# The mixer's projection by seven block products through DRAM, with two weight tiles' operands made later

## The chip, the cores and the metric

The kernel runs on one core of a Trainium2 chip. The metric is the device time of one execution in microseconds (us). The engines are named as in the profile: PE (TensorE), DVE (VectorE), ACT (ScalarE), POOL (GpSimd) and SP (SyncE, which here only issues DMAs).

## The reference

The kernel computes one decoder block on x of 1024 tokens by 1024 channels in float32, cut here to the part around the change:

```python
u = rms_norm(x, norm_mix)
u_ssm, q, k, v, f_logit, gate_logits = split(u @ w_in)
y = gelu(s5_ssm(u_ssm, ...))
a, b = split(y @ w_glu); out_a = a * sigmoid(b)
out_b = forgetting_attention(q, k, v, f_logit + b_forget) @ w_fox_o
gate_a, gate_b = split(sigmoid(gate_logits))
h = x + (gate_a * out_a + gate_b * out_b) @ w_mix_out        # the mixer
h = h + memory_cross_attention(rms_norm(h), rms_norm(mem), w_q, w_kv, w_o)
f_a, f_b = split(rms_norm(h) @ w_ffn_in)
h = h + (silu(f_a) * f_b) @ w_ffn_out
out = rms_norm(h, norm_final)
```

The mixer's projection is a product of a 1024 x 1024 matrix (the merged gates, called g below) and w_mix_out, 1024 x 1024. The forget-attention has 8 heads of 64 channels, the memory attention 4 heads over 256 memory tokens.

## The kernel before

Every product is made in fp32r with both operands split: `hi` is the rounded operand (an ACT cast), `lo` the rest (a subtraction on DVE, at places on POOL), and hi·hi + hi·lo + lo·hi are three matmuls. One matmul has a stationary tile of 128 x 128 and moves 512 columns.

The stages around the change run in this order. **Fox** (`Fox.run`) makes values, forget sums and the heads of the forget-attention. It stores the cumulated forget sums to `cum_d` (the high part `cch` and the low parts `cl`), and reads them back into the rows `hb` of each head's operands; the per-head weights `raw<-in_w_in` come in through a ring of four raw buffers of 128 x 1024 (`wpool`, tag `raw`). Ahead of these SP copies w_glu into `wg_d`. **GLU and w_fox_o** (`glu.rest(j)`, `fox_part(j)`, j = 0 to 7, each 128 channels): a fox_part has 2 halves of 512 tokens; PE multiplies the attention by w_fox_o, DVE multiplies the result by the gate `gb` and adds it to `sg`, which gives the merged row block g_j (channels in partitions), and the split of g_j gives `mT`. **Mixer** (`mix`): for each tile t of 128 tokens and each half of 512 output channels, 8 blocks of 128 channels times 3 matmuls go into one PSUM bank; DVE adds the bank to a half row of x and writes H[t]. The weights are split beside it. After mix(t, second half) for t = 4 to 7 come norm(0) to norm(3), which scale H[t] to `xs`, turn it by 8 PE transposes and split it into `u2`. Between the mixes the list `ahead(0..2)` is woven in: it makes operands for the feed-forward's weight tiles 1 to 3 (loads `wpr`, sums, splits `wph`/`wpl`) and stores them to `w_d` by DMAs that ACT issues. **Memory queries** (`mem_q`): 4 heads, 24 matmuls each for the first 512 tokens, with norm(4) to norm(7) woven in. The memory scores follow.

The feed-forward's output stage already multiplies by seven block products (Strassen's scheme): a 2 x 2 block matrix product by 7 products of sums of blocks, whose operands are stored to DRAM and read back raw, split on reading.

The functions write the work out in program order, and the tile framework's scheduler makes one fixed order of instructions per engine of it; `B.behind` holds an instruction behind another one. Each engine and each DMA queue works its own list in order; semaphores carry the dependencies. DMAs issued by SP use eight semaphores in turn, so that a DMA may wait until the one eight places before it has landed.

Of the kernel before, what the change touches and what calls it, by code (L numbers as in the profile page):

```python
# [19 lines left out]
P = 128  # L20
# [98 lines left out]
class Block:  # L119
# [190 lines left out]
def hybrid_block_kernel(ctx: ExitStack, tc: tile.TileContext, x, mem, norm_mix, w_in, b_forget,  # L310
# [30 lines left out]
    wg_d = B.dram.tile([4, P, 2 * D], F32, name="wg_d")  # L341
    glu = Glu(B, sh, yT, wg_d, gate_d)
    with tc.tile_pool(name="fox", bufs=1, reuse_waits="tile") as fp:
        fox = Fox(B, fp, sh, uT, w_in, b_forget[0], cum_d, rd_d, att_d)
        fox.run(y_d, yT, aT, w_glu, wg_d, [f for j in range(4) for f in glu.values(j)])
    glu.after = fox.maxima[NH - 2]
    with tc.tile_pool(name="st2", bufs=1, reuse_waits="tile") as s2:
        stage_tail(B, big, s2, sh, x, glu, aT, gate_d, kv_d, w_fox_o, w_mix_out, norm_mem_q[0], w_mem_q,
                   w_mem_o, norm_ffn[0], w_ffn_in, w_ffn_out, norm_final, out)
# [232 lines left out]
def stage_tail(B, big, s2, sh, x, glu, aT, gate_d, kv_d, w_fox_o, w_mix_out, g_mq, w_mem_q, w_mem_o, g_ffn,  # L582
# [18 lines left out]
    mT = Act(s2, "t", NS2, 8, L, name="mx")  # L601
    fox = {}

    def fox_part(j):
# [6 lines left out]
        for h in range(2):  # L611
# [6 lines left out]
            mh, ml = mT.rhs(j, h)  # L618
            merged.append(B.split(mh, ml, sg[:, cs]))

    merged = []
# [21 lines left out]
    def wslots(src, pool_lo):  # L643

        nk = src.shape[0] // P
        raw = B.wpool.tile([P, RAW], F32, tag="raw", bufs=4, name="raw")[:, :D]
        S.dma_start(raw.rearrange("p (k c) -> p k c", k=nk), src.rearrange("(k p) c -> p k c", p=P))
        hl = bslot(F32R, "wbh"), bslot(F32R, "wbl")
        B.split(*hl, raw, pool_lo)
        return [t_.rearrange("p (k c) -> p k c", k=nk) for t_ in hl]  # L650

    def mix_weights(c):

        wm = ([], [])
        for kk in range(4):
            if c == 0:
                hl = B.wblock(w_mix_out, 2 * kk, 2, 0, 512)
            else:
                hl = wslots(w_mix_out[2 * kk * P:(2 * kk + 2) * P, 512:D], False)
            for w_, t_ in zip(wm, hl):  # L660
                w_ += [t_[:, 0, :], t_[:, 1, :]]
        return wm

    def mix(t, c, wm):
        cs = slice(512 * c, 512 * c + 512)
        ps = B.bank()
        gemm_n(ps, mT, t, wm, 8)
        V.tensor_add(H[t][:, cs], ps, load(x[t * P:(t + 1) * P, cs], "xr"))

    def norm(t, gb, act):  # L670
        xs = s2.tile([P, D], F32, tag="xs", bufs=1, name="xs")
        B.norm_scale(xs, H[t], B.rstd(H[t]), gb)
        return B.norm_turn(xs, act, t)
# [6 lines left out]
    def ahead(j):  # L680
# [14 lines left out]
        def plain():  # L695
            hl, _ = pair(0)
            with B.behind(merged[-1]):
                B.split(*hl, pre[j][0])
# [37 lines left out]
    wm0 = mix_weights(0)  # L736
    with B.behind(merged[-1]):
        wm1 = mix_weights(1)
    mixes = [lambda t=t: mix(t, 0, wm0) for t in range(NT)] + [lambda t=t: mix(t, 1, wm1) for t in range(4)]
# [15 lines left out]
    weave([lambda h=h: mem_q(h, 0) for h in range(MH)], [lambda t=t: normed.append(norm(t, gq, u2)) for t in range(4, 8)])  # L755
# [252 lines left out]
    gs = {}  # L1008
# [569 lines left out]
class Fox:  # L1578
# [280 lines left out]
    def run(self, y_d, yT, aT, w_glu, w_d, filler):  # L1859
# [131 lines left out]
```

## Time and profile before

| what | value |
|---|---|
| median of 3 runs | 1540.81 us (1539.42 to 1541.27) |
| profiled execution, span | 1538.1 us |
| granted TensorE clock over the span | 0.999 |
| last gated tiles end, mixer starts (PE) | 679.81 us |
| mixer's last matmul, memory queries start | about 770.6 us |
| norm(7)'s transposes on PE | 795.33 to 796.36 us |
| DVE, ACT, POOL busy, share of the span | 65%, 43%, 16% |

The page of the profiled execution gives no time of its own beside the span; the span runs from the first to the last instruction, and the median of the runs is 2.7 us above it. In the timeline a row has its start in us, its length, the engine, the line of the program, the operation, the tile written and those read, the shapes, the number of instructions, and in brackets the idle time before it with what ended it. In a group's row stand the total busy time and the mean in ns, then the idle time before. In the windows each engine has its busy time in us and its number of instructions.

### The profile page before, as it was taken

What the parts mean: (1) busy time and instruction counts of PE and PEld (TensorE: products, weight loads), DVE (VectorE), ACT (ScalarE), POOL (GpSimd) and SP (SyncE); (2) the same over time, 40 slices, a digit from 0 to 9 for tenths busy, and PEclk for the clock granted to TensorE, in tenths of its full rate; (3) what the DMA queues carried; (4) which work ended last, traced back from release to release, by engine and by line L of the source; (5) the groups of instructions that cost most, each with busy time, mean ns of one, the idle gap of its engine ahead of it and who ended that gap; (6) DMA issues with size and microseconds to landing.
All of it is one profiled execution on the core that took longest, in us unless ns stands there. A gap on an engine that the chain in (4) does not pass through costs nothing. (4 is left out here: it accounts for less than half of the span.)

```text
span 1538.1 us, 20434 instructions
## 1 busy us (share of the span) xinstructions
PE 1520.7 (99%) x7329; PEld 1257.7 (82%) x7329; DVE 1005.7 (65%) x1828; ACT 658.1 (43%) x1183; POOL 253.6 (16%) x341
## 2 busy tenths in 40 slices
PE   8999999999999999999999999999999999999998
PEld 7888888898777678888888888888888888888886
DVE  7936554355878867675556797777777775675555
ACT  7423334324667643232435663333333333354343
POOL 1166542100121214100102200000000000101001
PEclk9999999999999999999999999999999999999999
DMA  9634556611223746378210356555544544896542
GB/s 286 161 104 102 131 128 144 180 41 16 50 46 88 192 131 198 111 218 308 89 69 1 117 204 210 162 161 160 158 158 157 157 145 139 291 391 220 192 163 110
DMA packets 196293, 234.06 MB, mean 152 GB/s; under 512 B 35576, under 2 KB 127656, under 8 KB 195680
## 3 DMA queue, kind: packets, MB, share of 16 engines
q1 hardware_dynamic: 188704, 214.93, 47.0%
q10 hardware_dynamic: 7488, 17.83, 3.1%
q8 instruction: 57, 0.93, 0.3%
q14 instruction: 44, 0.36, 0.1%
HBM read 161.94 MB, written 72.71 MB: 153 GB/s over the span
## 5 line engine op out<-in xcount | busy, mean ns | idle before, releaser
L184 DVE TENSOR_TENSOR wlo<-raw,whi 128x1024 fp32r<-128x1024 f32 (+2 forms) x120 | 126.3, 1058 | 45.4 <-ACT whi L183 44.2
L183 ACT CAST whi<-raw 128x1024 fp32r<-128x1024 f32 (+2 forms) x120 | 108.7, 910 | 105.6 <-PE mm L174 39.1
L184 DVE TENSOR_TENSOR ol<-or,oh 128x1024 fp32r<-128x1024 f32 x73 | 90.1, 1236 | 74.0 <-ACT oh L183 71.9
L173 PE MATMUL mm<-uh,whi 128*128 128x512 f32 x344 | 136.5, 397 | 0.0
L174 PE MATMUL mm<-ul,whi 128*128 128x512 f32 x344 | 135.1, 393 | 0.0
L175 PE MATMUL mm<-uh,wlo 128*128 128x512 f32 x344 | 134.5, 391 | 0.0
L183 ACT CAST oh<-or 128x1024 fp32r<-128x1024 f32 x73 | 76.9, 1054 | 105.0 <-PE mm L1108 34.2
L997 POOL TENSOR_TENSOR g<-a,c 128x512 f32<-128x512 f32 x22 | 35.7, 1621 | 389.0 <-ACT a L996 389.0
L175 PEld LDWEIGHTS mm<-uh,wlo 128*128 128x128 f32 x344 | 64.7, 188 | 13.3 <-DVE wlo L184 0.2
L1803 POOL TENSOR_TENSOR pl<-pf,ph 128x512 fp32r<-128x512 f32 (+1 forms) x32 | 36.8, 1152 | 232.5 <-DVE ph L1802 193.3
L173 PEld LDWEIGHTS mm<-uh,whi 128*128 128x128 f32 x344 | 64.8, 188 | 11.6
L174 PEld LDWEIGHTS mm<-ul,whi 128*128 128x128 f32 x344 | 64.8, 188 | 11.0
L1800 ACT ACTIVATE pf<-sc 128x512 f32<-128x512 f32 (+1 forms) x96 | 46.4, 489 | 44.5 <-DVE sc L1796 28.3
L986 DVE SCALAR_TENSOR_TENSOR c<-c,pv 128x512 f32<-128x512 f32 x22 | 15.1, 687 | 76.5 <-ACT c L985 76.4
L211 POOL TENSOR_TENSOR r<-ms,mhalf 128x1 f32<-128x1 f32 (+1 forms) x26 | 15.7, 605 | 298.6 <-DVE ms L207 258.5
L964 PE MATMUL pv<-S3h,we 128*128 128x512 f32 x176 | 57.7, 389 | 0.0
L1806 DVE TENSOR_TENSOR pl<-pf,ph 128x512 fp32r<-128x512 f32 (+2 forms) x64 | 35.3, 553 | 10.4 <-ACT ph L1805 9.8
L1108 PE MATMUL mm<-ol,oh 128*128 128x512 f32 (+1 forms) x110 | 41.9, 381 | 0.0
L1108 PE MATMUL mm<-oh,ol 128*128 128x512 f32 (+1 forms) x110 | 41.9, 381 | 0.0
L1108 PE MATMUL mm<-oh 128*128 128x512 f32 (+1 forms) x110 | 41.9, 381 | 0.0
L173 PE MATMUL sc<-uh,whi 128*128 128x512 f32 x104 | 40.8, 392 | 0.0
L173 PE MATMUL mm<-yh,whi 128*128 128x512 f32 x104 | 40.7, 392 | 0.0
(639 smaller groups left out, 4554.2 us busy)
## 6 DMA issues: line engine op xcount, KB each, us to landing
or<-c_d SPq DMA_DIRECT2D x77, 256.0 KB
wo<-in_w_ffn_out_dram SPq DMA_DIRECT2D x22, 512.0 KB
c_d<-g SPq DMA_DIRECT2D x44, 256.0 KB
t_d<-wo SPq DMA_DIRECT2D x44, 256.0 KB
or<-t_d SPq DMA_DIRECT2D x44, 256.0 KB
rawb<-in_w_ffn_in_dram SPq DMA_DIRECT2D x20, 512.0 KB
raw<-in_w_ffn_in_dram SPq DMA_DIRECT2D x20, 512.0 KB
raw<-in_w_in_dram SPq DMA_DIRECT2D x19, 512.0 KB
```

The source lines that it names most:

```text
L173: T.matmul(ps, lh, rh, start=first, stop=False)
L174: T.matmul(ps, lh, rl, start=False, stop=False)
L175: return T.matmul(ps, ll, rh, start=False, stop=last)
L183: cast = self.A.copy(hi, src)
L184: self.rest = (self.G if pool_lo else self.V).tensor_sub(lo, src, f32(hi))
L211: self.G.tensor_tensor(out=r, in0=v, in1=self.mhalf[:, 0:n], op=ALU.pow)
L964: T.matmul(ps, l_[:, k, :], r_, start=first and k == 0 and i == 0, stop=k == 3 and i == 2, skip_group_check=True)
L997: G.tensor_mul(g[:, 512:], a1, c1)
L1108: T.matmul(ps, l_[:, gi], r_[:, c0:c1], start=k == 0 and (p == NP - LAST if own else p == 0 and n in (1, 2, 7)), stop=p == NP - 1 and k == ...
L1800: self.exp = A.activation(pf[:, off:], ps[:, off:], AF.Exp)
L1803: G.tensor_sub(pl[:, off:], pf[:, off:], f32(ph[:, off:]))
L1806: self.left = V.tensor_sub(pl[:, off:], pf[:, off:], f32(ph[:, off:]))
```

## The change

The mixer's product is divided into 2 x 2 blocks: tokens 0 to 511 and 512 to 1023, even and odd blocks of 128 channels (a pair p is the blocks 2p and 2p+1), and output channels 0 to 511 and 512 to 1023. Seven products n of 4 pairs x 4 token tiles x 3 matmuls replace the eight. They go in the order 1, 6, 7, 5, 4, 2, 3; a step `m` is one product and one pair, 12 matmuls into four PSUM banks, and behind a product's fourth pair DVE adds its four banks into H (product 2 goes tile by tile). Below m0 is product 1 with pair 0, m3 product 1 with pair 3.

- The left operands (1, 2, 4 are blocks of g; 3, 5, 6, 7 sums of blocks, made by four DVE operations per pair in `merged_pair`) are stored raw to `mc_d` and read back; the splits into mT are gone.
- The right operands 4 to 7 are sums of weight blocks. `mix_sums` makes them at the start of `Fox.run`: 8 loads of 512 KB, 16 POOL additions of 128 x 512 and 16 stores of 256 KB to `mt_d`. The operands 1 to 3 are read from w_mix_out.
- `m_get` reads both operands of a step (256 KB each) into one raw buffer; ACT casts it as a whole, DVE makes the left operand's low half, POOL the right one's. It goes five steps ahead.
- H[t] is loaded with x (8 loads of 512 KB), in place of 16 half rows.
- ahead(0) stays beside the mixer. ahead(1) and ahead(2) move to the memory queries, between norm(4) and norm(7).

The first place is SP at the start of Fox. The rows are DMAs, target and source, with their shapes and the semaphores that they wait for (DMAHW is a DMA's landing). Before:

```order
L1891 DMA wg_d_2966<-in_w_glu_dram 128x1x2048 [waits DMAHW6_49]
L1663 DMA cum_d_81<-cch_3411 8x1024 [waits DMAHW7_49,Activation_49]
L1668 DMA cum_d_81<-cl_3414 8x512 [waits DMAHW0_49,DVE_49]
L1668 DMA cum_d_81<-cl_3417 8x512 [waits DMAHW1_49,DVE_49]
L1701 DMA raw_3599<-in_w_in_dram 128x8x64 [waits DMAHW2_49]
L1702 DMA raw_3599<-in_w_in_dram 128x8x64 [waits DMAHW3_49]
L1741 DMA hb_3267<-cum_d_81 2x1024 [waits DMAHW4_49,DMAHW1_49,DMAHW7_49,DMAHW0_49,Pool_49]
```

In the change, from the last wg_d on (the first rows of 24), and further down up to the cl stores:

```order
L1973 DMA wg_d_2966<-in_w_glu_dram 128x1x2048 [waits DMAHW6_49]
L588 DMA wmix_3308<-in_w_mix_out_dram 128x1024 [waits DMAHW7_49,DVE_49]
L588 DMA wmix_3309<-in_w_mix_out_dram 128x1024 [waits DMAHW0_49,DVE_49]
L588 DMA wmix_3320<-in_w_mix_out_dram 128x1024 [waits DMAHW1_49,DVE_49]
L592 DMA mt_d_2967<-wmix_3308 128x512 [waits DMAHW7_49,DMAHW2_49,Pool_49]
L592 DMA mt_d_2967<-wmix_3308 128x512 [waits DMAHW3_49,Pool_49]
L592 DMA mt_d_2967<-wmix_3309 128x512 [waits DMAHW4_49,DMAHW0_49,Pool_49]
L592 DMA mt_d_2967<-wmix_3309 128x512 [waits DMAHW5_49,Pool_49]
L588 DMA wmix_3321<-in_w_mix_out_dram 128x1024 [waits DMAHW6_49,DVE_49]
```

```order
L588 DMA wmix_3345<-in_w_mix_out_dram 128x1024 [waits DMAHW3_49,DMAHW2_49]
L592 DMA mt_d_2967<-wmix_3344 128x512 [waits DMAHW6_49,Pool_49]
L1745 DMA cum_d_81<-cch_3460 8x1024 [waits Activation_49]
L592 DMA mt_d_2967<-wmix_3344 128x512 [waits DMAHW5_49,Pool_49]
L592 DMA mt_d_2967<-wmix_3345 128x512 [waits DMAHW2_49,Pool_49]
L592 DMA mt_d_2967<-wmix_3345 128x512 [waits DMAHW7_49,Pool_49]
L1750 DMA cum_d_81<-cl_3463 8x512 [waits DMAHW0_49,DVE_49]
L1750 DMA cum_d_81<-cl_3466 8x512 [waits DMAHW1_49,DVE_49]
```

Loads and stores of the weight sums now stand between wg_d and the cl stores; the reads of hb come behind them.

The second place is DVE and PE at the mixer's start. `sg` and `gb` belong to fox_part, `s3` and `s24` to merged_pair, `moh` and `mol` are a step's high and low operands. DVE in the change, around the end of the gated tile 5 (its second half's multiply is the row with misc) and the start of tile 6 (the last row):

```order
L647 SCALAR_TENSOR_TENSOR s24_6772<-sg_6264 128x512 [waits DVE_49]
L629 TENSOR_TENSOR gb_6768<-gb_6768,misc_6755 128x512 [waits DMAHW7_49,DMAHW4_49,PE_49]
L684 TENSOR_TENSOR mol_6788<-raw_6784,moh_6787 128x512 [waits Activation_49]
L630 TENSOR_TENSOR sg_6384<-sg_6384,gb_6768 128x512 [waits DVE_49]
L684 TENSOR_TENSOR mol_6796<-raw_6792,moh_6795 128x512 [waits Activation_49]
L648 SCALAR_TENSOR_TENSOR s24_6772<-s24_6772,sg_6384 128x512 [waits DVE_49]
L684 TENSOR_TENSOR mol_6804<-raw_6800,moh_6803 128x512 [waits DMAHW4_49,Activation_49]
L184 TENSOR_TENSOR wlo_6815<-raw_6812,whi_6814 128x1024 [waits DMAHW6_49,Activation_49]
L629 TENSOR_TENSOR gb_6831<-gb_6831,pv_6818 128x512 [waits DMAHW0_49,PE_49]
```

and PE in the change, where m2 gives way to tiles 6 and 7:

```order
L693 MATMUL sc_6853<-moh_6803 128x512 [waits Activation_49]
L693 MATMUL sc_6853<-mol_6804,moh_6803 128x512 [waits Pool_49]
L693 MATMUL sc_6853<-moh_6803,mol_6804 128x512 [waits DVE_49]
L693 MATMUL sc_6854<-moh_6803 128x512
L693 MATMUL sc_6854<-mol_6804,moh_6803 128x512
L693 MATMUL sc_6854<-moh_6803,mol_6804 128x512
L693 MATMUL mm_6855<-moh_6803 128x512
L173 MATMUL pv_6818<-ath0_0_2955,whi_6814 128x512 [waits Activation_49]
```

Before, the tiles came first and the mixer whole behind them. Now m0, m1 and seven matmuls of m2 stand ahead of the 48 matmuls of tiles 6 and 7, the five others behind them, and then m3.

The third place is DVE at the end of the mixer. The four adds of the last product are the rows with h4 to h7; `u2l` is norm 3's split, `wpr` and `wpl` belong to ahead(1), `xs` of h4 is norm 4:

```order
L700 TENSOR_TENSOR h6_6720<-h6_6720,mm_6855 128x512 [waits PE_49]
L700 TENSOR_TENSOR h7_6721<-h7_6721,mm_6856 128x512 [waits PE_49]
L184 TENSOR_TENSOR u2l0_0_6730<-pv_7623,u2h0_0_6722 128x2x128 [waits Activation_49]
...
L789 TENSOR_TENSOR wpr_7673<-wpr_7673,wpr_7674 128x512 [waits DVE_49]
L184 TENSOR_TENSOR u2l3_0_6736<-pv_7632,u2h3_0_6728 128x2x128 [waits Activation_49]
...
L184 TENSOR_TENSOR wpl_7800<-wpr_7673,wph_7799 128x512 [waits Activation_49]
L231 SCALAR_TENSOR_TENSOR xs_7704<-h4_6718,r01_7709,gbc_6963 128x1024 [waits DVE_49]
```

Before, an add of one H and the split and xs of an earlier norm took turns there. Now four adds come in a row, and pieces of ahead(1) stand between the splits of norm 3 and the xs of norm 4.

The diff, cut to its core:

```diff
+    mt_d = B.dram.tile([8, 4, P, 512], F32, name="mt_d")
...
-        fox.run(y_d, yT, aT, w_glu, wg_d, [f for j in range(4) for f in glu.values(j)])
+        fox.run(y_d, yT, aT, w_glu, wg_d, [f for j in range(4) for f in glu.values(j)],
+                [lambda p=p: mix_sums(B, w_mix_out, mt_d, p) for p in range(4)])
...
+def mix_sums(B, w, mt_d, p):
+    w1, w2 = [B.wpool.tile([P, RAW], F32, tag="raw", bufs=4, name="wmix")[:, :D] for _ in range(2)]
+    for i, t_ in enumerate((w1, w2)):
+        B.S.dma_start(t_, w[(2 * p + i) * P:(2 * p + i + 1) * P, :])
+    b11, b12, b21, b22 = w1[:, :512], w1[:, 512:], w2[:, :512], w2[:, 512:]
+    for n, o, i in ((5, b11, b12), (7, b12, b22), (6, b22, b11), (4, b21, b22)):
+        B.G.tensor_add(o, o, i)
+        B.S.dma_start(mt_d[n, p], o)
...
-            mh, ml = mT.rhs(j, h)
-            merged.append(B.split(mh, ml, sg[:, cs]))
+        gs[j] = sg
+        if j % 2 == 0:
+            S.dma_start(mc_d[1, j // 2], sg[:, 512:])
+        else:
+            merged_pair(j // 2)
+
+    def merged_pair(p):
+        ge, go = gs.pop(2 * p), gs.pop(2 * p + 1)
+        a21, a11, a22, a12 = ge[:, :512], ge[:, 512:], go[:, :512], go[:, 512:]
+        s24, s3 = slot(name="s24"), sh.half("s3")
+        for n, a_ in ((2, a12), (4, a22)):
+            S.dma_start(mc_d[n, p], a_)
+        V.tensor_sub(s3, a11, a21)
+        V.tensor_sub(a21, a22, a21)
+        V.scalar_tensor_tensor(out=s24[:, :512], in0=a21, scalar=-1.0, in1=a11, op0=ALU.mult, op1=ALU.subtract)
+        V.scalar_tensor_tensor(out=s24[:, 512:], in0=s24[:, :512], scalar=-1.0, in1=a12, op0=ALU.mult,
+                               op1=ALU.subtract)
+        for n, a_ in ((6, s24[:, :512]), (7, s3), (5, a21), (3, s24[:, 512:])):
+            S.dma_start(mc_d[n, p], a_)
...
+    MORDER = (1, 6, 7, 5, 4, 2, 3)
+    mseq = [(n, p) for n in MORDER for p in range(4)]
+    def m_get(m):
+        n, p = mseq[m]
+        r_ = B.wpool.tile([P, RAW], F32, tag="raw", bufs=4, name="raw")[:, :D]
+        S.dma_start(r_[:, :512], mc_d[n, p])
...
+        S.dma_start(r_[:, 512:], src)
...
+        A.copy(hl[0], r_)
+        V.tensor_sub(hl[1][:, :512], r_[:, :512], f32(hl[0][:, :512]))
+        G.tensor_sub(hl[1][:, 512:], r_[:, 512:], f32(hl[0][:, 512:]))
+        mops[m] = hl
...
+    MAHEAD = 5
+    fox_part(5)
+    for m in range(3):
+        m_get(m)
+    for t in range(4, NT):
+        m_x(t)
+    fox_part(6)
+    m_step(0)
+    m_get(3)
+    m_get(4)
+    m_step(1)
+    for t in range(4):
+        m_x(t)
+    fox_part(7)
+    m_get(5)
+    m_get(6)
...
-    weave(mixes, [f for j in range(AHEAD_IN + 1) for f in ahead(j)], 4)
-    for t in range(4, NT):
-        mix(t, 1, wm1)
-        norm(t - 4, gq, u2)
+    weave([lambda m=m: m_next(m) for m in range(2, 20)], ahead(0), 4)
+    last = [lambda i=i: (m_tile(i), m_next(20 + i)) for i in range(4)] + [lambda m=m: m_step(m) for m in range(24, 28)]
+    weave(last, [lambda t=t: norm(t, gq, u2, ("pv", "pv")) for t in range(4)])
...
-    weave([lambda h=h: mem_q(h, 0) for h in range(MH)], [lambda t=t: normed.append(norm(t, gq, u2)) for t in range(4, 8)])
+    later = [f for j in range(1, AHEAD_IN + 1) for f in ahead(j)]
+    for f in later[:1]:
+        f()
+    turns = [lambda t=t: normed.append(norm(t, gq, u2)) for t in range(4, 8)]
+    weave([lambda h=h: mem_q(h, 0) for h in range(MH)],
+          [f for i in range(4) for f in turns[i:i + 1] + later[1 + 3 * i // 2:1 + 3 * (i + 1) // 2]])
```

More of the change, by code (lines that the diff above doesn't have):

```diff
@@ L641, in gemm_n, with norm @@
             B.mm3(ps, ah, al, w[0][k], w[1][k], k == 0, k == nk - 1)
[L643 to L670, printed above, removed]
+    def norm(t, gb, act, banks=("misc", "pv")):
         xs = s2.tile([P, D], F32, tag="xs", bufs=1, name="xs")
         B.norm_scale(xs, H[t], B.rstd(H[t]), gb)
-        return B.norm_turn(xs, act, t)
+        return B.norm_turn(xs, act, t, banks)
     AHEAD_IN = 2
@@ L696, in plain @@
             hl, _ = pair(0)
-            with B.behind(merged[-1]):
-                B.split(*hl, pre[j][0])
+            B.split(*hl, pre[j][0])
             for i, t_ in enumerate(hl):
```

75 lines of the change are left out of this document (59 added, 16 removed).

## The prediction

> **What bounds the kernel now.** I read the page's busy table and slices first.
>
> ```profile
> span 1538.1 us, 20434 instructions
> PE 1520.7 (99%) x7329; PEld 1257.7 (82%) x7329; DVE 1005.7 (65%) x1828; ACT 658.1 (43%) x1183; POOL 253.6 (16%) x341
> ...
> PEclk9999999999999999999999999999999999999999
> ```
>
> TensorE (PE) is busy for 99% of the span and its clock is granted in full in every slice; a microsecond taken from PE's own work is a microsecond of the kernel, unless something else is late there. So a change is worth the matmuls that it removes, less the new time in which PE stands still. Next I read the windows over the stages that the change touches (PE, PEld, DVE, ACT and POOL busy, clock, DMA share, GB/s) and one step of the chain of waits.
>
> ```profile
> 308.00:346.00 38.00, 38.00 (x267) 35.43 (x266) 19.54 (x56) 10.98 (x20) 0.00 (x0) 1.00 0.15 37
> 640.00:680.00 40.00, 40.00 (x178) 33.14 (x177) 29.12 (x37) 11.36 (x17) 6.00 (x4) 1.00 0.55 171
> 700.00:740.00 40.00, 40.00 (x178) 33.14 (x177) 20.88 (x30) 12.43 (x19) 0.56 (x1) 1.00 0.85 299
> 771.00:797.00 26.00, 25.92 (x131) 21.50 (x130) 13.32 (x29) 8.17 (x23) 0.55 (x1) 1.00 0.13 45
> 1346.00:1384.00 38.00, 38.00 (x169) 31.45 (x169) 27.77 (x27) 21.52 (x26) 2.51 (x2) 1.00 1.05 391
> 1054.62 2.72 PE mm L964 x12
> ```
>
> PE idles nowhere here: at the start of the forget-attention (308 to 346), beside the last gated tiles (640 to 680), in the mixer (700 to 740), among the memory queries (771 to 797). Twelve matmuls of 128x512 take 2.72 us, 0.2267 us each. The output stage (1346 to 1384) already does what the mixer is to do, seven products from DRAM, at 391 GB/s and without a gap.
>
> **What the change removes.** The mixer had 8 token tiles x 2 halves x 8 k x 3 = 384 matmuls; seven products x 4 pairs x 4 tiles x 3 are 336. 48 x 0.2267 = **10.9 us** of PE go. The 32 transposes stay, and so does every other matmul. Of the 16 merged splits, whose work was off PE's path, nothing is won.
>
> **Steady mixer: 0.** One step (12 matmuls, 2.72 us) needs two reads of 256 KB, one ACT cast of 128x1024, a half subtraction on DVE and one on POOL, and on average one DVE add into H.
>
> ```profile
> 709.24 1.05 ACT L183 CAST wph<-wpr 128x1024 fp32r<-128x1024 f32 x1 [7.31 <-DMA wpr<-in_w_ffn_in_dram]
> L986 DVE SCALAR_TENSOR_TENSOR c<-c,pv 128x512 f32<-128x512 f32 x22 | 15.1, 687 | 76.5 <-ACT c L985 76.4
> L1803 POOL TENSOR_TENSOR pl<-pf,ph 128x512 fp32r<-128x512 f32 x24 | 30.9, 1289 | 78.5 <-DVE ph L1802 73.0 <-DVE mboth L1776 5.6
> L1252 POOL TENSOR_TENSOR sg<-sg,ga 128x512 f32<-128x512 f32 x16 | 25.7, 1628 | 77.0 <-DVE sg L1245 49.8 <-DMA ga<-gate_d 27.2
> L1445 POOL TENSOR_TENSOR w<-la_re,cT_re 128x512 f32<-128x512 f32 x4 | 4.4, 1111 | 0.2
> ```
>
> That is 1.05 us of ACT, 2 x 0.69 = 1.4 of DVE and 1.3 to 1.6 of POOL in 2.72, and 524 KB / 2.72 us = 193 GB/s, under the 299 that the mixer's window moves now and the 391 of the output stage. PE's own step hides it; if that cover went (four raw buffers, each held for a read plus 1.05 + 1.3 us, feed a step in 2.72 us only while the read stays under 8.5 us), it would cost a rival's price, below. Taking the weights of feed-forward tiles 2 and 3 away from here makes it lighter, and I give that no gain since PE had no idle time there.
>
> **Place A, the start of the forget-attention: +5.3.** SyncE (SP) issues in order. It now has 8 loads of w_mix_out and 16 stores to mt_d between wg_d and the stores of cum_d that hb is read from. The first rows below are SP's, then DVE's, POOL's and PE's.
>
> ```profile
> 301.74 1.78 SPq L1891 DMA_DIRECT2D wg_d<-in_w_glu_dram  x2
> 339.96 0.87 SPq L1668 DMA_DIRECT2D cum_d<-cl  x2
> 342.14 0.26 SPq L1741 DMA_DIRECT2D hb<-cum_d  x1
> 343.39 0.24 SPq L1742 DMA_DIRECT2D hb<-cum_d  x1
> 322.31 1.23 DVE L184 TENSOR_TENSOR wlo<-raw,whi 128x1024 fp32r<-128x1024 f32 x1
> 374.71 0.74 POOL L1803 TENSOR_TENSOR pl<-pf,ph 128x256 fp32r<-128x256 f32 x1 [82.30 <-DVE ph L1802]
> 351.21 0.22 PE L1763 MATMUL pv<-hb 68*128 68x128 f32 x1
> 1.67 0.36 SPq L370 DMA_DIRECT2D xt<-in_mem_dram  x1
> 5.91 1.06 ACT L413 ACTIVATE junk<-xt 128x1024 bf16<-128x1024 f32 x1 [0.77 <-DMA xt<-in_mem_dram]
> 723.60 0.38 SPq L731 DMA_DIRECT2D wpr<-in_w_ffn_in_dram  x1
> 730.44 1.05 ACT L183 CAST wph<-wpr 128x1024 fp32r<-128x1024 f32 x1 [4.95 <-DMA wpr<-in_w_ffn_in_dram]
> ```
>
> SP was free from 303.5 on and POOL idle until 374.71, so pair 0 costs nothing. But its tiles come from the ring of four raw buffers, and pair 1's second load needs a buffer that DVE's split frees at 322.31 + 1.23 = 323.5. From there three pairs run one behind another: the second load of a pair stands on SP behind the stores of the pair before, lands 4.2 us later (5.91 - 1.67; under load 730.44 - 723.60 = 6.8), three POOL additions must follow it, and about 0.5 us of issues. An addition of this shape lies between 1.11 (L1445) and 1.63 (L1252); I take their mean, 1.37. A pair is 4.2 + 3 x 1.37 + 0.5 = 8.8, the last store goes at 323.9 + 3 x 8.8 = 350.3, and the two cl stores behind it. As before, the last hb read is issued 343.6 - 340.0 = 3.6 us later, at 353.9, and takes about 2.6 (an estimate, between the 2.2 from cum_d<-cl to hb<-cum_d and the 3.2 from rd_d to rb below). PE, whose order up to there is the same, wants hb at 351.2: 356.5 - 351.2 = 5.3. The ends: 3.6 us a load and 1.11 an addition give 7.3 a pair and +0.9; 6.8 and 1.63 give 12.2 a pair and +15.5. The DMA share of 0.15 puts it near the lower loads. Below nothing it can't go, since PE waits for nothing there now. Behind hb on SP stand the head weights (raw<-in_w_in), which PE needs later.
>
> [...]
>
> **Place B, the start of the mixer: +5.9.** PE now runs m0, m1 and part of m2 ahead of the last gated tiles 6 and 7, and m3 right behind them.
>
> ```profile
> 573.96 0.32 SPq L1838 DMA_DIRECT2D rd_d<-rc  x1
> 577.16 0.47 SPq L1840 DMA_DIRECT2D rb<-rd_d  x1
> 599.73 0.32 SPq L597 DMA_DIRECT2D gb<-gate_d  x1
> 601.94 0.69 DVE L616 TENSOR_TENSOR gb<-gb,pv 128x512 f32<-128x512 f32 x1 [3.23 <-DMA gb<-gate_d]
> ```
>
> A store and the read that waits for it are 3.2 us apart (577.16 - 573.96). A 256 KB read is used 2.2 us after the last issue of its kind (601.94 - 599.73), and one of twice the size after 4.2; I take 2.9. Tile 6's second half ends 26 matmuls (5.9 us) into the run of 48; its multiply and add (2 x 0.69) end at 7.3, the read of its mc_d piece is issued at 10.5 and lands at 13.4, ACT's cast ends at 14.4, POOL's half at 15.7. PE is through with the 48 and the rest of m2 (53 x 0.2267) at 12.0, and can do 0.7 us of high parts before it needs POOL's half: 2.4 + 0.6 = 3.0. Before that, m0's low half stands on DVE behind the last multiply of tile 5 (2 x 0.69 = 1.4, of which PE has 0.9 to do: 0.7 with the hop), and the last w_fox_o load stands on SP behind a store that waits for tile 5's add: +0.8. Behind m3, m4 and m5 reuse the banks that four DVE adds (2.8 us) must empty, with two subtractions among them: +1.4. Sum 5.9. Low 2.5 (m3 alone, every transfer as short as the rows have it), high 12 (both reads at 6.8). Late next is nothing: m7 comes just in time, and from there the steady step has room to catch up.
>
> [...]
>
> **Place C, the memory queries: +1.7.** H[4] to H[7] used to be complete one by one; now all four wait for the last product.
>
> ```profile
> 769.77 0.69 DVE L668 TENSOR_TENSOR h<-mm,xr 128x512 f32<-128x512 f32 x1 [1.68 <-PE mm L175]
> 778.24 0.41 DVE L184 TENSOR_TENSOR u2l<-misc,u2h 128x256 fp32r<-128x256 f32 x1
> 778.57 1.27 DVE L231 SCALAR_TENSOR_TENSOR xs<-h,r,gbc 128x1024 f32<-128x1024 f32 x1
> ...
> L184 DVE TENSOR_TENSOR wpl<-wpr,wph 128x512 fp32r<-128x512 f32 x8 | 5.4, 685 | 7.9 <-DMA w_d<-wph 7.9
> L184 DVE TENSOR_TENSOR wpl<-wpr,wph 128x1024 fp32r<-128x1024 f32 x3 | 3.7, 1223 | 9.9 <-ACT wph L183 9.9
> ```
>
> DVE has four adds of 0.69 at the end of the last product and only behind them u2l of norm 3 (0.41): 3.2 us. PE wants it after 8 transposes and 4 matmuls, 1.8 us: +1.4. Then xs of norm 4 is ready after those 3.2 us, three pieces of u2l (1.2), two additions and two subtractions of the moved operands (4 x 0.69), some small ones and its own 1.27, about 8.7; PE, pushed back by 1.4, wants it 27 matmuls and 8 transposes after the last product (7.0) and so at 8.4: +0.3. The moved operands are two of the three tiles behind the two wpl rows, the second of them only in part: about half of 5.4, two of the three of 1.22 and five additions of 0.69 on DVE, 8.6 us in all, and as many casts on ACT; DVE's 13.3 us and ACT's 8.2 in the 26 us of this window leave room for them. Low 0.3 if DVE's queue is ahead; high 4.8 if a moved subtraction waits for a buffer of a w_d store as long as the 4.95 above, less what is in time.
>
> **Sum.** -10.9 + 0 + 5.3 + 5.9 + 1.7 = **+2.0 us**; the profiled span would be 1540.1. The median of the runs is 1540.8, 2.7 above the profiled span: **1543 us**, a little slower, within what can be told from nothing (0.2%, 3.1 us).
>
> **Rivals.**
> 1. *The new chains are all hidden.* Then -10.9 stands: 1530. For it: in the output stage the same step leaves no gap, and POOL and SP are idle around 310 to 340. Against it: three places where rows give a wait on PE's path. With two of the three places small (0.9 + 2.5 + 0.3) it is -7.2 and 1533.6.
> 2. *Only one of A and B stalls*, the other at its low end: -10.9 + 5.3 + 2.5 + 1.7 = -1.4 or -10.9 + 0.9 + 5.9 + 1.7 = -2.4: about 1539.
> 3. *Slower: the pairs' weight sums hold SP.* One mechanism at A: every further 0.9 us per pair is 2.7 us on hb; from 9.2 us a pair on, the sum is slower by over 0.2%. With the load of 6.8 and POOL at 1.63 it is +15.5, and the sum +12.2: 1553. For it: POOL's addition at 1.63 is the nearest in form. Against: DMA share 0.15.
> 4. *Slower: reads of the mixer's steps outlast 8.5 us* when loads of H, operands of tile 1 and w_d stores run beside them; a read of 10 gives 3.1 a step, 0.4 x 20 steps = 8 us, 1551. Against: 391 GB/s in the output stage.
> 5. *The change doesn't do what it says*, the count of matmuls not falling: 28 steps of 12 stand in the code against 384, so I give it nothing.
>
> **Chances.** Forecast (the sum, 1537 to 1549) 0.45; rival 1 0.22; rival 2 0.13; rival 3 0.12; rival 4 0.08. Faster by more than 0.2% (under 1537.7): all of rival 1, half of rival 2, a little of the forecast, 0.31. Slower (over 1543.9): rivals 3 and 4 and half of the forecast, 0.40. The rest, 0.29, is no change that can be measured. Range 1530 to 1554: from rival 1's end to just over rival 3's.
>
> **What would show it.** The page of the changed kernel should list 48 matmuls fewer and a PE busy time lower by 10.9. In the waits, PE L1763's counterpart should wait some 5 us for DMA hb near 351 (none: A was hidden; 10 or more: rival 3). PE's mixer steps should wait for ACT and POOL moh, mol within the first eight steps, 3 us at m3. Behind that, windows of the mixer with PE not full mean rival 4. Near the end of the mixer, PE should wait for DVE u2l and xs, under 2 us. What would make it wrong: SP issuing cum_d before 345, or a landing under 2 us.

## The result, and the profile after

The changed kernel takes 1568.3 us (median of 4 runs, 1563.4 to 1570.5) against 1540.1 before (4 runs, 1539.4 to 1541.3): a ratio of 1.0177, 95% interval 1.0159 to 1.0195. It is slower by 28 us where the sum of the prediction had 2. The profiled execution spans 1567.1 us. Its page:

```profile
span 1567.1 us, 20655 instructions
PE 1521.8 (97%) x7281; PEld 1253.3 (80%) x7281; DVE 1044.5 (67%) x1860; ACT 668.4 (43%) x1187; POOL 324.6 (21%) x385
```

PE has 48 matmuls fewer (7281 against 7329), as the change says. They were worth 10.9 us, yet PE's busy time has risen by 1.1: the matmuls that are left count 12 us more. The rest is waiting. The groups of PE's waits, over the whole program (total, times, longest):

```profile
PE mm L693 <- DVE h L700: 7.1, 1, 7.1
PE pv L1845 <- DMA hb<-cum_d: 5.4, 1, 5.4
PE misc L237 <- DVE u2l L184: 4.1, 1, 4.1
PE sc L693 <- DVE mol L684: 2.8, 2, 2.4
PE sc L693 <- ACT moh L683: 2.8, 1, 2.8
PE misc L1740 <- DVE logf L1727: 2.7, 1, 2.7
...
PE sc L693 <- POOL mol L685: 0.9, 1, 0.9
```

These seven sum to 25.8 us; a few shorter ones in the mixer and the queries (L693 and L237, 0.2 to 0.6 each) add 1.1. None of them was there before. So the span's +29.0 is, to 1.0 us: -10.9 removed, +26.9 of waits, +12.0 in PE's busy time. Of these 12, some 7.4 are a lower granted clock, right behind four of the waits (below and in the last section); the rest is not placed, but part of it is how busy time counts: a matmul ahead of a stop counts 0.39 us (the last ahead of the 7.1 us, at 756.07), one with the next behind it 0.2267. Windows of the mixer in the changed kernel (length, then busy time of PE, PEld, DVE, ACT and POOL, clock, DMA share, GB/s):

```profile
712.00:756.00 44.00, 43.21 (x187) 34.45 (x186) 39.98 (x45) 20.29 (x22) 26.88 (x16) 1.00 0.91 301
756.00:764.00 8.00, 0.91 (x4) 0.51 (x3) 4.68 (x7) 4.52 (x5) 7.40 (x6) 0.83 0.89 269
764.00:769.00 5.00, 5.00 (x15) 3.86 (x15) 3.98 (x10) 4.76 (x13) 2.13 (x2) 0.59 1.06 310
```

PE's own timeline where it starts again (start, duration, operation, in brackets the wait ahead of it and its releaser):

```profile
763.55 0.77 PE L693 MATMUL mm<-whi 128*128 128x512 f32 x1 [7.09 <-DVE h L700]
764.12 0.63 PE L693 MATMUL mm<-wlo,whi 128*128 128x512 f32 x1
764.55 0.63 PE L693 MATMUL mm<-whi,wlo 128*128 128x512 f32 x1
```

From 712 to 756 the steps run nearly full. Then PE stands for 7 us, and when it goes on its granted clock is 0.59: the starts are 0.43 us apart (764.55 - 764.12), not 0.2267, until 768.0. This wait thus cost some 2 us more than its length.

What PE waited for there is DVE, in its own timeline, beside POOL's and SP's:

```profile
752.90 4.09 DVE L684 TENSOR_TENSOR wlo<-raw,whi 128x512 fp32r<-128x512 f32 x3
757.55 1.11 DVE L684 TENSOR_TENSOR mol<-raw,moh 128x512 fp32r<-128x512 f32 x1 [0.56 <-ACT moh L683]
759.86 0.69 DVE L684 TENSOR_TENSOR mol<-raw,moh 128x512 fp32r<-128x512 f32 x1 [1.20 <-ACT moh L683]
762.12 0.69 DVE L684 TENSOR_TENSOR mol<-raw,moh 128x512 fp32r<-128x512 f32 x1 [1.57 <-ACT moh L683]
762.73 0.68 DVE L700 TENSOR_TENSOR h<-h,mm 128x512 f32<-128x512 f32 x1
...
751.14 6.97 POOL L685 TENSOR_TENSOR wlo<-raw,whi 128x512 fp32r<-128x512 f32 x4 [2.17 <-ACT whi L683]
...
752.99 0.32 SPq L670 DMA_DIRECT2D raw<-mc_d  x1
...
754.77 0.32 SPq L670 DMA_DIRECT2D raw<-mc_d  x1
```

The adds into H (L700) that free product 2's bank stand in DVE's list behind the low halves of three later steps, m24 to m26, whose operands only come in. DVE is not busy all that time: it waits 0.56, 1.20 and 1.57 us for ACT's casts, and ACT for the reads. The reads of m24 and m25 go at 752.99 and 754.77, just as POOL's halves of m20 and m21 (1.74 us each, 6.97 / 4) end and give their raw buffers back. And a low half of 128x512 on DVE, 0.69 us, takes 1.36 on the mean of the first row (4.09 / 3).

### The profile page after: what moved, and what is told of

It reads as the page before. It is cut to its first block, busy times and chain, and to the rows that moved or that the text cites. A ratio compares the mean times of both kernels' runs of the same rounds, so it can differ in the third digit from the quotient of the medians.

```text
span 1567.1 us, 20655 instructions
## 1 busy us (share of the span) xinstructions
PE 1521.8 (97%) x7281; PEld 1253.3 (80%) x7281; DVE 1044.5 (67%) x1860; ACT 668.4 (43%) x1187; POOL 324.6 (21%) x385
## 4 chain that ended last, share of the span: by engine, by line
PE 81%; DVE 8%; DMA 5%; ACT 2%; issue 2%; POOL 1%; SPq 0%; POOLq 0%; DVEq 0%; ACTq 0%
PE mm L1047 15%; PE pv L1047 8%; PE mm L173 7%; PE mm L174 7%; PE mm L175 7%; PE mm L1190 5%; PE sc L1047 4%; PE sc L1190 4%; PE pv L1190 3%; PE sc L175 3%; PE sc L174 3%; PE sc L173 3%; PE misc L1190 2%; DMA wpr<-in_w_ffn_in_dram 1%; PE sc L1875 1%
## 5 line engine op out<-in xcount | busy, mean ns | idle before, releaser
L184 DVE TENSOR_TENSOR wlo<-raw,whi 128x1024 fp32r<-128x1024 f32 (+2 forms) x116 | 122.4, 1060 | 40.4 <-ACT whi L183 39.6
L183 ACT CAST whi<-raw 128x1024 fp32r<-128x1024 f32 (+2 forms) x116 | 104.8, 907 | 99.2 <-PE mm L174 36.4
L685 POOL TENSOR_TENSOR mol<-raw,moh 128x512 fp32r<-128x512 f32 x24 | 40.1, 1686 | 40.8 <-ACT moh L683 40.6
L683 ACT CAST moh<-raw 128x1024 fp32r<-128x1024 f32 x24 | 25.0, 1050 | 51.6 <-DMA raw<-mc_d 26.8
```

Of the source, the lines that this page charges most:

```text
L183: cast = self.A.copy(hi, src)
L184: self.rest = (self.G if pool_lo else self.V).tensor_sub(lo, src, f32(hi))
L685: G.tensor_sub(hl[1][:, 512:], r_[:, 512:], f32(hl[0][:, 512:]))
```

## The experiments

Each is one execution with its profile unless said otherwise, beside the kernel before on the same chip. The changed kernel's own runs spread over 7 us, so a difference in total under that is not told from nothing, and the waits of the profile are what is compared.

**e1, the weight sums left out** (products 4 to 7 then read plain blocks of w_mix_out).

```diff
-                [lambda p=p: mix_sums(B, w_mix_out, mt_d, p) for p in range(4)])
+                [])
-            src = mt_d[n, p]
+            src = w_mix_out[2 * p * P:(2 * p + 1) * P, :512]
```

> The weight sums are left out: products 4 to 7 read plain blocks of w_mix_out (the right operands of four products are not sums, so the time holds and the values don't). Theory A (the sums on SP and POOL cost 10.9 us at the start of the forget-attention: logf 2.9, hb 5.6, slower matmuls behind them, the rest before): PE reaches the first attention matmul of w_fox_o within 2 us of the kernel before (592.8 to 594.8 in place of 603.7), no wait for logf or hb, and the total falls by 9 to 10 us against the changed kernel, to about 1558. Rival (the two waits come from something else, say the tile framework's order there): the waits stay and the total stays at 1568.

1555.7 us. PE reaches the first matmul of the attention by w_fox_o at 593.3 (592.8 before, 603.7 in the change); the waits for logf and hb are gone. Of the 10.4 us, 1.0 was there before the first of the two waits (PE was to come to logf's transposes at 336.7 in the change, at 335.7 in e1). So the sums cost some 9 us at the start of the forget-attention, as theory A has it. The mixer's wait in front of product 2 stays in e1 and e3, at 8.2 and 8.5 us: it has another cause.

**e2, the sums' transfers issued by POOL; e3, the transfers on SP and no POOL additions.**

```diff
 e2:
-        B.S.dma_start(mt_d[n, p], o)
+        B.G.dma_start(mt_d[n, p], o)
 e3:
-        B.G.tensor_add(o, o, i)
```

(In e2 the loads go the same way; in e3 mt_d then holds plain blocks.)

> The 8 loads and 16 stores of the weight sums are issued by POOL and not by SP; the additions stay on POOL. Theory A1 (two separate causes: SP's order holds cum_d and hb, 5.4 us; POOL's additions slow DVE's logf chain, 2.7 us): the wait for hb is gone (below 1 us), the wait for logf stays at 1.5 to 3 us; total about 1562. Rival A2 (the landing of the 24 transfers, not their place on SP, makes hb late): the wait for hb stays at 4 to 6 us. Rival A3 (DVE's logf chain is late by SP or by DMA, not by POOL): the logf wait goes too, total about 1558.

> The sums' loads and stores stay on SP, the 16 POOL additions are left out, so mt_d holds plain blocks (values are off, the transfers are the same). Theory A1: DVE's logf chain is as fast as before (the seven L1724 steps in 1.8 us, not 4.4) and the wait for logf is gone; hb, now 3 x 4 us earlier per chain of pairs, waits under 1 us; total about 1558. Rival A3 (logf is slowed by the transfers): the seven steps stay at 4 us and the logf wait at 2 to 3 us.

e2: 1574.0 us, worse, with the wait for hb at 6.7 us and the one for logf at 2.5. Its place on SP was free, but now another list was full: the small constant `ones` that DVE's scan of the forget sums reads is set by POOL, behind POOL's transfers and additions.

```profile
353.05 0.52 POOL L1736 MEMSET ones<- 8x512 f32 x1
353.60 1.21 DVE L1741 TENSOR_TENSOR_SCAN cum<-ones,misc 8x512 f32<-8x512 f32 x1 [12.90 <-POOL ones L1736]
```

So e2 does not tell A1 from A2 as it was meant to; it shows that the pairs' chain holds whatever is queued behind it. e3: 1555.0 us, waits of 0.8 us for hb and none for logf, with all 24 transfers still ahead of the cl stores on SP, which go at 345.3 there (354.2 in the change). A3 is out. The seven steps of DVE's logf chain in the timeline of the kernel before (start, and their time together):

```profile
330.34 1.77 DVE L1642 SCALAR_TENSOR_TENSOR logf<-logf 128x64 f32<-128x64 f32 x7
```

In the change, with POOL's additions at the same time:

```profile
334.49 4.38 DVE L1724 SCALAR_TENSOR_TENSOR logf<-logf 128x64 f32<-128x64 f32 x7
...
332.50 5.25 POOL L591 TENSOR_TENSOR wmix<-wmix 128x512 f32<-128x512 f32 x4 [3.21 <-DMA wmix<-in_w_mix_out_dram]
```

In e3:

```profile
330.51 1.77 DVE L1723 SCALAR_TENSOR_TENSOR logf<-logf 128x64 f32<-128x64 f32 x7
```

They take 4.4 us while POOL's additions run, without them 1.8, as in the kernel before.

**e4, the operands of tiles 2 and 3 moved, and nothing else of the change** (the kernel before with `weave(mixes, ahead(0), 4)` and the rest of `ahead` among the memory queries).

> The kernel before with only the second half of the change: operands of weight tiles 2 and 3 among the memory queries. Theory C (the cast of tile 3 stands on ACT ahead of norm 6's casts and waits for a load that gets its buffer late: 4.1 us and 0.6 of slow clock behind it): PE waits 3 to 5 us among the memory queries and the total is 3 to 6 us over the kernel before, about 1544 to 1546. Rival (the move costs only because all of H[4] to H[7] come at once at the mixer's end): under 1 us, total 1540 to 1541.

1541.1 against 1538.7 beside it; the profile shows no new wait among the queries, and PE reaches the feed-forward 1.3 us later than before, 0.8 of which are there at 335 us already. The rival was nearer: the move alone costs no wait that the profile shows.

**e8, the move undone in the changed kernel** (`ahead(0)` to `ahead(2)` all beside the mixer).

> The seven products with the operands of weight tiles 2 and 3 back beside the mixer: the first half of the change alone. Theory C1 (the wait of 4.1 us among the memory queries is the late load of tile 3, standing on ACT ahead of norm 6's casts): it goes, and the mixer, with more on DVE and ACT and two more loads a tile, waits 0 to 6 us longer; total 1563 to 1571. Rival C2 (the wait comes from H[4] to H[7] ending together): it stays at 2 to 4 us.

1583.4 us, 15 more than the change. The wait for u2l at the tile-3 load is gone (C1), but the wait for h before product 2 is 10.7 us, and waits for the norms come up at the mixer's end (3.9 for rt, 3.0 for u2l, 3.2 in two for xs). Given seven products, the move is worth 15 us; its own cost is small beside that.

**e5, DVE's order alone; e6, DVE makes both low halves.**

```diff
 e5:
-        V.tensor_sub(hl[1][:, :512], r_[:, :512], f32(hl[0][:, :512]))
+        with B.behind(adds.get(4) if m > 23 else None):
+            V.tensor_sub(hl[1][:, :512], r_[:, :512], f32(hl[0][:, :512]))
 e6:
-        G.tensor_sub(hl[1][:, 512:], r_[:, 512:], f32(hl[0][:, 512:]))
+        V.tensor_sub(hl[1][:, 512:], r_[:, 512:], f32(hl[0][:, 512:]))
```

> Only DVE's order: the low halves of steps m24 to m27 stand behind product 4's four adds into H. Theory B1 (PE's 7.1 us before product 2 come from those adds standing on DVE behind the low halves of m24 to m26, which wait for raw buffers): the wait for h falls from 7.1 to 1 to 2 us (the adds go when m23's half is through, some 1 us after product 4's end), the slow clock behind it goes too (2 us), and the total falls by 6 to 9 us to about 1560. Rival B2 (PE would wait there for product 2's own operands or for the reads anyway): the wait changes its name to whi or wlo and the total stays at 1566 to 1569.

> In the mixer DVE makes both low halves and POOL none. Theory B3 (POOL's subtractions of 1.7 us hold DVE's operations on SBUF from 0.69 to 1.4 to 1.8 us, so that POOL's help costs DVE as much as it saves): DVE's low halves take 0.69 each, the waits of the mixer (h 7.1, mol 3.7, moh 2.8) fall to under 9 us in all, total 1556 to 1562. Rival B4 (DVE, with 2.8 us of work in a step of 2.72, becomes the bound): PE waits longer for mol, total 1570 or more.

e5: 1566.9 us. The wait for h falls only to 4.4 us (5.4 in two), not to 1 or 2. The halves of m20 to m23 are through at 757.6, 0.2 us after PE stops; what stands ahead of the adds there is a split of ahead(0), which waits 1.4 us for its cast and takes 2.05 (1.22 on the mean in the kernel before):

```profile
759.01 2.05 DVE L184 TENSOR_TENSOR wpl<-wpr,wph 128x1024 fp32r<-128x1024 f32 x1 [1.41 <-ACT wph L183]
760.98 0.67 DVE L701 TENSOR_TENSOR h<-h,mm 128x512 f32<-128x512 f32 x1
```

So DVE's order is a part of the loss. e6: 1557.2 us, 11 less than the change. In the window below DVE does 25 halves more and is through sooner. The groups of DVE and POOL from 690 to 800 us of the change (number, busy time, mean ns of one, idle time ahead of them):

```profile
L684 DVE TENSOR_TENSOR mol<-raw,moh 128x512 fp32r<-128x512 f32 x21 | 20.0, 967 | 7.5 <-ACT moh L683 6.8 <-issue 0.7
L700 DVE TENSOR_TENSOR h<-h,mm 128x512 f32<-128x512 f32 x12 | 8.0, 680 | 0.5 <-PE mm L693 0.5
L184 DVE TENSOR_TENSOR wpl<-wpr,wph 128x512 fp32r<-128x512 f32 x6 | 7.2, 1221 | 0.0
...
L685 POOL TENSOR_TENSOR mol<-raw,moh 128x512 fp32r<-128x512 f32 x21 | 34.8, 1674 | 33.0 <-ACT moh L683 32.8
```

The same groups of e6:

```profile
L684 DVE TENSOR_TENSOR mol<-raw,moh 128x512 fp32r<-128x512 f32 x21 | 14.4, 685 | 7.6 <-ACT moh L683 7.6
L685 DVE TENSOR_TENSOR mol<-raw,moh 128x512 fp32r<-128x512 f32 x21 | 14.3, 683 | 0.0
L184 DVE TENSOR_TENSOR wpl<-wpr,wph 128x512 fp32r<-128x512 f32 x7 | 4.7, 683 | 0.0
```

And PE's wait for h in e6, from the groups of its waits (total, times, longest):

```profile
PE mm L693 <- DVE h L700: 1.2, 1, 1.2
```

With POOL at work a DVE half takes 0.97 us and a wpl half 1.22, without it 0.69 each. The adds L700, which read PSUM, take 0.68 in both. POOL's own half takes 1.67. B3 holds: the wait for h goes from 7.1 to 1.2 us. The program's order is the same, but the scheduler's has moved a little: in e6 the adds stand behind DVE's halves of m24 and m25, not of m26 too. m26's cast ends 1.0 us after the first add has begun, and its half takes 0.7, so that this explains less than 2 of the 5.9 us (an estimate from e6's rows).

**e7, all gated tiles ahead of m0; e13, tile 6's second half first.** In e7 `fox_part(7)` stands in front of `m_step(0)`; e13 is on top of e6, and stores the half at once.

```diff
 e13:
-        for h in range(2):
+        for h in ((1, 0) if j == 6 else (0, 1)):
```

> All eight gated tiles before step m0 in the program, so that m0 to m2 cover the way of tile 6's block through DRAM. Theory B5 (m3 waits 4.3 us since its block is stored, read and cast behind the last tiles): the waits for moh and mol at the mixer's start fall from 6.6 to under 3 us and the total by 3 to 6 us, about 1563. Rival B6 (PE then waits for the last w_fox_o weights or gates, which m0 and m1 covered): a wait for whi or wlo of 3 us or more, total unchanged.

> As e6 (DVE makes both low halves, sums on POOL in their old place), and gated tile 6 makes its second token half first and stores it at once. Theory B5 again (m3 waits since its block, tile 6's second half, goes through DRAM behind the last tiles): the block is ready 12 matmuls (2.7 us) earlier, the wait for moh of 2.3 us at the mixer's start goes to under 0.5 us, and so does the slow clock behind it (1 to 2 us); total 1553 to 1555 against 1557.2. Rival B8 (m3's read is held by SP or by the raw buffers and not by its block): the wait stays at 2 us, total 1556 to 1558.

e7: 1571.7 us, the wait for moh at m3 is 3.8 us, not less, and m0's stays at 2.4; the wait for h before product 2 is 11.1. This form of the idea failed and says nothing on the cause. e13: the wait of 2.3 us for moh in front of m3 in e6 is gone, so its block's way through DRAM was the cause of it (B5). The total, 1555.9, is 1.3 under e6, not 2 to 4: a wait of 1.9 us for moh before product 2 has taken its place.

**e9, no POOL at all** (e6 with one operation of 128x1024 a step, and e1's leaving out); **e10, sums on DVE in head 1 of the forget-attention; e11, m0 and m1 read earlier; e12, the adds first, both on top of e10 with one subtraction a step.**

> Both POOL parts out: DVE makes both low halves of a step in one operation of 128x1024, and the weight sums are left out (products 4 to 7 read plain blocks, so values are off). Theory P (POOL beside DVE is behind most of the loss: 10.4 us at the start of the forget-attention and 11.8 in the mixer, each seen alone): the two add up, 1568 - 22 = about 1546, and 5 to 8 us over the kernel before remain, the waits for m0 and m3 and the slow clock behind them. Rival Q (the two hide each other in part, or another wait takes their place): 1552 or more.

> A whole kernel: DVE makes both low halves, and the weight sums are made by DVE too and in head 1 of the forget-attention, where SP's queue and the DMA are idle. Theory P: the waits for logf and hb at 335 and 355 are gone, the sums' 16 x 0.69 us of DVE cost PE 0 to 4 us in the heads; total 1546 to 1551. Rival R (sums cost what they cost wherever they are, since the scheduler puts their transfers ahead of the rows that the heads wait for): PE waits 5 us or more for hb or mc in the heads, total 1553 or more.

> As e10, with one subtraction of 128x1024 a step, and the reads of m0 and m1 ahead of gated tile 5. Theory B7 (m0's 2.5 to 2.9 us come from its low half standing on DVE behind the adds of tile 5): with the operands of m0 ready earlier the first wait of the mixer falls under 1 us and the total is 1 to 3 us below e10. Rival: the wait goes to m1 or m2, total as e10.

> As e10, with one subtraction a step, and the low halves of m24 to m27 behind product 4's adds into H. Theory B1: with POOL out of the way the order alone decides the wait before product 2; it falls from 1.2 to under 0.5 us, total 1 to 2 us below e10. Rival: the wait goes to xs or to moh a little later, total as e10.

e9: 1550.9 us, between the two theories: the start of the forget-attention is that of the kernel before, but the wait for h is 3.8 us, more than in e6. POOL has no part in it: the adds stand on DVE behind the low halves of m24 and m25, as in e6, and DVE waits 3.4 us for m24's cast first. Why it is longer than in e6 is not told apart. e10: 1554.9, rival R: PE reaches the w_fox_o matmuls 9.1 us later than before, with waits of 3.3 and 2.0 us for mc, DVE's row maxima in the heads. e11 and e12: 1559.6 and 1559.8; in e11 the wait for m0 turned into one for moh of 2.5 us, with 1.8 at m3; in e12 the wait for h was 2.4. Neither order helped.

**e14, e6 with the sums on DVE beside gated tiles 1 to 4; e15, e14 with e13's half** (`mix_sums(B, w_mix_out, mt_d, j - 1)` behind `glu.rest(j)`, with `B.V.tensor_add`).

> As e6, with the weight sums on DVE and beside the gated tiles 1 to 4 (where DVE is busy for 70% and PE waits for nothing). Theory S (the sums cost what they delay at their place, and nothing where DVE, SP and the buffers have room): the start of the forget-attention is that of the kernel before (0 to 1 us), the gated tiles take as long as before, total 1546 to 1549. Rival S2 (the raw buffers and SP's queue hold up the gated tiles' weights): PE waits 5 us or more for whi or gb there, total 1552 or more.

> e13 and e14 together: a whole kernel without POOL in the change, sums beside the gated tiles, tile 6's second half first. By theories B5, P and S the total is 1542 to 1546, 0.1 to 0.4% over the kernel before. By their rivals 1550 or more.

e14: 1551.7 us. hb is reached 0.1 us later than before, so here the sums cost the forget-attention nothing; but the gated tiles lose 2.0 us in a wait for sg and 2 more, so the truth is between the two. e15: 1551.7 us (median of 4 runs, 1548.2 to 1556.2) against 1540.8, a ratio of 1.0082, interval 1.0063 to 1.0101. It wins back over half of the loss and is still slower than before. Its waits beside and in the mixer:

```profile
PE mm L695 <- ACT moh L685: 2.3, 1, 2.3
PE mm L173 <- DVE sg L1323: 2.2, 1, 2.2
PE sc L695 <- DVE mol L687: 2.1, 1, 2.1
PE sc L695 <- ACT moh L685: 1.3, 2, 0.8
PE mm L173 <- ACT u2h L183: 1.2, 1, 1.2
```

No run beat the kernel before.

## Why the prediction was wrong

The sum was -10.9 + 0 + 5.3 + 5.9 + 1.7 = +2.0. Two slips in the working change nothing of what follows: 3.6 + 3 x 1.11 + 0.5 is 7.4 a pair and not 7.3, so that the low end of place A is +1.2 (the 3.6 is the first load of 512 KB in the kernel before, xt<-in_mem_dram, issued at 0.81 and first read by ACT at 4.42), and the chances of slower add to 0.425, not 0.40.

**-10.9, the removed matmuls: right in number.** Their worth was lost again in PE's busy time, +12 us, of which some 7.4 are its granted clock behind the waits: a term that the sum did not have.

**"Steady mixer: 0" is the step that failed.** It added ACT, DVE and POOL up one by one (1.05, 1.4, 1.3 to 1.6 us in a step of 2.72) and found each within the step. Two things were missing. DVE and POOL are not independent: beside each other, DVE's low halves took 0.97 us on the mean and up to 1.80, POOL's 1.67. The 0.69 for DVE was read from L986, an operation that takes `pv` from a PSUM bank, of the kind that stayed at 0.68 beside POOL. And the step was taken as if DVE's operations could go in any order: DVE, busy for 40.0 of the 44 us from 712 to 756, has the adds that free PE's banks in one list behind low halves of later steps, whose reads go when POOL gives the raw buffers back. The cost was 7.1 us at one place, and 2 us of slow clock behind it. e6 takes POOL away and has 1.2 us there; e5 changes DVE's order and has 4.4; e9, without POOL, still has 3.8. So both parts are shown, but not how the 7.1 us divide between them. Rival 4 put a loss at this place, but on reads that outlast 8.5 us; the reads of m20 to m27 were cast 3.5 to 5.6 us after their issue. The output stage, taken as the proof that the steady step is hidden, has POOL busy for 2.5 of 38 us, here it is 26.9 of 44. The clue was in the kernel before, at an earlier stage:

```profile
265.56 1.74 POOL L1529 TENSOR_TENSOR m<-zim,ES 128x512 f32<-128x512 f32 x1 [24.77 <-ACT zim L1525]
...
266.07 1.78 DVE L1531 TENSOR_TENSOR m<-zre,ES 128x512 f32<-128x512 f32 x1
267.78 0.68 DVE L1532 TENSOR_TENSOR m<-m,m 128x512 f32<-128x512 f32 x1
```

**Place A, +5.3: the path was right, the number is luck.** The wait for hb measured 5.4 us. But hb landed at 361.4, where 356.5 was forecast, and PE came to it at 356.1, where 351.2 was forecast: two errors of 4.9 us that cancel. SP, DVE and the landing of hb in the change (the last row is of the chain that ended last):

```profile
324.05 2.24 SPq L592 DMA_DIRECT2D mt_d<-wmix  x4
...
351.06 3.06 SPq L592 DMA_DIRECT2D mt_d<-wmix  x3
354.20 0.67 SPq L1750 DMA_DIRECT2D cum_d<-cl  x2
...
345.18 2.39 DVE L1749 TENSOR_TENSOR cl<-cum,cch 8x512 fp32r<-8x512 f32 x2 [1.12 <-ACT cch L1744]
...
356.57 4.82 DMA hb<-cum_d
```

DVE has cl ready at 347.6, but SP stores it at 354.2, behind the last stores of the sums: SP's place held it, as forecast. The last two pairs took 8.8 and 8.4 us (their stores end at 336.9, 345.7 and 354.1), as forecast. "Pair 0 costs nothing" was wrong: its four stores stand on SP ahead of pair 1's second load and go only from 324.05 on, and the first of the three pairs took 13.0 us from 323.9. And a read of hb took 4.8 us to land, not 2.6. PE came late by 2.0 us that were there before the logf transposes (336.7 against 334.7; such a difference also comes and goes between the runs, 0.8 in e4) and by a wait of 2.7 us for logf that no term had; its cause is again POOL beside DVE (e3). With the slow matmuls behind hb, PE was 10.9 us late at the end of the forget-attention. "Below nothing it can't go" and the end at +15.5 held. e2 freed SP but put the same chain ahead of `ones` on POOL, so it says nothing against SP's place; e3 kept SP's order, and with a shorter chain the wait fell to 0.8.

**Place B, +5.9.** Waits of 2.4 for m0, 2.8 + 0.9 for m3 and its halves, and 0.9 in three behind: 7.0. m3 was forecast at 3.0 and measured 3.7, by its mechanism: e13 moves it away by having the block 2.7 us earlier. m0 was mis-sized, 2.4 against 0.7: among the operations still ahead of its half on DVE were two of merged_pair (L646 and L647, 0.69 each), which the forecast didn't count. DVE had lost 1.3 us just before, beside POOL's halves (1.07 and 1.63 us for 0.69); that POOL makes m0 late is not shown, since e6 waits 2.7 us there with DVE making both halves. The 0.8 for the w_fox_o weights didn't come. The 1.4 for the banks of m4 and m5 came to 0.2. "Late next is nothing" was wrong, as above.

**Place C, +1.7.** The wait is another one: 4.1 us for u2l of norm 6, with 0.6 before and some slow clock. It was priced at 4.8 at most, on a w_d store that a subtraction waits for. What came was the load of tile 3: it got its buffer late, landed late, and the cast that waits for it stands on ACT ahead of norm 6's casts.

```profile
804.19 0.38 SPq L809 DMA_DIRECT2D wpr<-in_w_ffn_in_dram  x1
...
812.93 1.05 ACT L183 CAST wph<-wpr 128x1024 fp32r<-128x1024 f32 x1 [6.46 <-DMA wpr<-in_w_ffn_in_dram]
813.88 0.37 ACT L183 CAST u2h<-misc 128x256 fp32r<-128x256 f32 x1
```

In e4, where the mixer is the old one, the same code has no such wait; in e8, without the move, it is gone too; in e1, e2 and e3 it is 1.8 to 1.9 us. So it takes both the move and the new mixer before it.

**The rivals.** Rival 3 had the sign and one of the places, with a pair at 10.1 us on the mean of the three (its mark was 9.2); the larger loss, in the mixer, it did not have. The range ended at 1554 since no cost of DVE was taken from a row with POOL beside it, and no wait was given a slow clock.

**What stays open.** In e15, about 9.5 us of waits are left in the mixer and the queries, spread over m0, the steps behind the last tiles, product 2 and the norms, with some 1.8 us of slow clock around m0 (a granted clock of 0.96 from 640 to 680 and 0.99 from 680 to 700). Whether a larger ring of raw buffers or another order of the products ends them wasn't tried.

## What to carry to other kernels

Before work is given to a second engine to relieve a first, look in the trace for a stretch where both run and read the first one's durations there: its share of busy time does not show what they cost each other (here 0.97 us on the mean for a DVE half with POOL at work, 0.69 without). Where an engine's list mixes operations that free a bank with operations that wait for a load, a late load stops PE through the bank, here for 7.1 us; and on a PE-bound kernel a longer wait is to be priced with the slow matmuls behind it: in the change about 2 us behind each wait of 4 us and more, none behind those of 2.4 and 2.7 us.

## What the runs showed of the hardware

DVE and POOL held each other up where both worked on SBUF: in the change DVE's low halves of 128x512, with two SBUF operands, took from 0.68 to 1.80 us (L684) and POOL's from 1.29 to 1.83, 1.67 on the mean from 690 to 800 (L685; 1.29 is the mean of the same shape at L1803 in the kernel before), while DVE's adds with an operand in PSUM stayed at 0.67 to 0.69 (L700). In these two pairs the one that begins later is the long one, and it ends 0.5 and 1.2 us behind the other:

```profile
735.52 1.30 POOL L685 TENSOR_TENSOR mol<-raw,moh 128x512 fp32r<-128x512 f32 x1 [1.59 <-ACT moh L683]
735.59 1.77 DVE L684 TENSOR_TENSOR mol<-raw,moh 128x512 fp32r<-128x512 f32 x1
...
747.13 0.69 DVE L684 TENSOR_TENSOR mol<-raw,moh 128x512 fp32r<-128x512 f32 x1 [0.19 <-ACT moh L683]
747.17 1.80 POOL L685 TENSOR_TENSOR mol<-raw,moh 128x512 fp32r<-128x512 f32 x1 [0.78 <-ACT moh L683]
```

The prediction did not weigh this.

PE's granted clock fell to 0.59 behind the wait of 7.1 us, to 0.65 and 0.79 behind those of 5.4 (hb) and 4.1 (u2l), and to 0.72 from 706 to 712, behind waits of 2.8 and 0.9; behind m0's 2.4 us alone and logf's 2.7 it stayed at 1.00 (680 to 700, 330 to 345). Each of the four stretches is worth 1.7 to 2.1 us (its length times what its clock lacks to 1.00).

```profile
361.40:367.00 5.60, 5.47 (x17) 4.55 (x18) 2.35 (x9) 1.18 (x2) 0.00 (x0) 0.65 0.60 46
706.00:712.00 6.00, 5.28 (x15) 3.89 (x16) 4.30 (x5) 2.61 (x3) 5.02 (x4) 0.72 0.56 211
813.90:822.00 8.10, 6.29 (x23) 5.26 (x24) 5.20 (x9) 2.47 (x8) 0.00 (x0) 0.79 0.64 222
```

Behind the 7.1 us the matmuls' starts were 0.43 us apart against 0.2267, for 4.4 us. The waits of 2.8 and 0.9 us, with three matmuls between them, had a granted clock of 0.72 behind them, those of 2.4 and 2.7 us had 1.00; in e6 it was 0.91 over the window from 680 to 700, in which PE stands for 2.7 us (17.27 of 20 us busy). So the runs show no one length of wait from which the clock falls.

A load of 512 KB issued by POOL landed after 4.6 us in the median and a store of 256 KB after 2.3 (e2's DMA issues: target and source, queue, number, KB, median us to landing):

```profile
wmix<-in_w_mix_out_dram POOLq DMA_DIRECT2D x8, 512.0 KB, 4.6
mt_d<-wmix POOLq DMA_DIRECT2D x16, 256.0 KB, 2.3
```

The prediction's 4.2 for the load was near.
